# Layer 1's FFN down projection as seven products of halves in three groups, in a two-layer decoder kernel

## The chip, the cores and the metric

The kernel runs on one core of a Trainium2 chip. The metric is device time in microseconds of one execution, the median of several runs. All numbers of the trace come from one execution of the kernel, taken by the hardware profiler.

## The reference

Two decoder layers on 512 tokens of width 1024, float32. Each layer has a mixer (four parallel branches, lifted, gated and summed, then an output projection with a residual) and a feed-forward network (FFN). The change concerns the FFN of the second layer (layer 1), above all its last product:

```python
hf = rmsnorm(x, norm_ffn)
gate, up = jnp.split(hf @ ffn_w_up, 2, axis=-1)      # 1024 -> 2 x 2816
return x + (jax.nn.silu(gate) * up) @ ffn_w_down     # 2816 -> 1024
```

## The kernel before

**Precision.** Every large product is made of three matmuls: each operand is split into a high part (`_hi`, a rounded copy made by ScalarE, ACT) and a low part (`_lo`, the difference, made by VectorE, DVE), and `mm3` (L271, matmuls on L274 to L276) adds hi x hi, hi x lo and lo x hi into one PSUM bank. Weights come from DRAM by the queue of SyncE (SP) into two raw tiles of 128 x 2048 (`w_raw`). `Chunk` (L212) issues the load and splits it into parts of 128 x 1024; `w_hi` and `w_lo` have three buffers each, so that the splits run at most three parts ahead of TensorE (PE). PSUM's eight banks are three `mm`, three `tr` and two `at`.

**The FFN** (`ffn`, L1058) works in two parts: hidden columns 0 to 1535 (six chunks of 256) and 1536 to 2815 (five chunks). For each chunk, `features` computes gate and up with the weights as the stationary operand and the 512 tokens streaming; DVE scales the banks by the norm `r_b`, ACT applies Silu, DVE multiplies, and the result is split into `a_hi`, `a_lo` (L1087, L1088): twelve or ten k-tiles of 128 hidden columns. Then the part's down projection follows, so the stages of an FFN are up 0, down 0, up 1, down 1.

**Down projections.** In layer 0, and in part 0 of layer 1, `residual` (L1020) computes two output blocks of 128 columns at a time, with weights stationary, and adds the banks to `xT`, the residual stream in transposed form, which stays in SBUF from the mixer's output projection on. In part 0 of layer 1 the finished `xT` is also transposed by PE into `x_tok` (`transposed`, L1064). In part 1 of layer 1, `final` (L1043) has tokens as the output's partitions: `a` is stationary, 512 weight columns stream, four banks hold four tiles of 128 tokens, and the banks are added to `x_tok` and written out, the last 512 columns in halves on the SP and ACT queues.

**Order.** Each engine works through its own queue in order. The order in each queue was fixed when the program was built: instructions are placed as their inputs become ready by the builder's plan, those under `tc.high_priority` first (the splits of weights have `AHEAD`), and dependencies added by hand (`add_manual_dep`) are kept. The pool of `w_raw` has two buffers, so a load waits until both parts of the load two before it are split.

Of the kernel before, what the change touches and what calls it, by code (L numbers as in the profile page):

```python
# [12 lines left out]
F32 = mybir.dt.float32  # L13
# [8 lines left out]
P = 128  # L22
# [47 lines left out]
def hybrid_trunk(ctx: ExitStack, tc: tile.TileContext, x, mem, positions, norm_mix, w_in, conv_w,  # L70
# [43 lines left out]

    ident = consts.tile([P, P], F32, name="ident")
# [11 lines left out]
    neg = consts.tile([P, P], F32, name="neg")  # L127
# [143 lines left out]
    def mm3(ps, a, b, first, last):  # L271
        ah, al = a
        bh, bl = b
        pe.matmul(ps, ah, bh, start=first, stop=False)  # L274
        pe.matmul(ps, ah, bl, start=False, stop=False)  # L275
        pe.matmul(ps, al, bh, start=False, stop=last)  # L276
# [26 lines left out]
    def column_means(ps, ones, sq, hi, lo):  # L303
        A(hi, sq, AF.Copy)
        dve.tensor_sub(lo, sq, f(hi))
        pe.matmul(ps, ones, hi, start=True, stop=False)
        pe.matmul(ps, ones, lo, start=False, stop=True)

    def norm_feature(ssq):
        ps = tr_ps()  # L310
        column_means(ps, ones_dr, ssq, *(scratch512(S).bitcast(F32R) for _ in range(2)))
        r = state.tile([P, S], F32, name="rstd", bufs=1)
        rstd(r, ps, scratch512(S), scratch512(S))
        return r
# [170 lines left out]
    ones_dr = consts.tile([P, P], F32R, name="ones_dr")  # L485
    dve.tensor_copy(ones_dr, ones_d)
# [8 lines left out]
    mx, e0, e1, sm, z0 = (small(H4, name=f"lb{i}", bufs=1) for i in range(5))  # L495
# [20 lines left out]
    def mixer(l, h, norms, cm, cf):  # L516
# [176 lines left out]
        with pool_("dsa") as dp:  # L693
# [46 lines left out]
            with pool_("idx") as ip:  # L740
# [83 lines left out]
                def select(t):  # L824
# [12 lines left out]
                    dve.copy_predicated(score[:, t * P:], future, neg)  # L837
# [23 lines left out]
                mgp = cf.enter_context(pool_("mgp", "left"))  # L861
# [142 lines left out]
        res = cf.enter_context(tc.tile_pool(name="res", bufs=1))  # L1004
# [13 lines left out]
        return h2, ssq2, xT  # L1018

    def residual(xT, w2d, a, kt, cols, h2, ssq2, gain, spill=False, done=None):  # L1020
        for m0 in range(0, KD, cols // P):
            ws = []
            k0 = 0
            per = 2048 // cols
            while k0 < kt:
                n = min(per, kt - k0)
                ws.append((k0, n, wchunk(w2d[k0 * P:(k0 + n) * P, m0 * P:m0 * P + cols], n, cols)))
                k0 += n
            pss = [mm_ps() for _ in range(cols // P)]
            for js in ([range(cols // P)] if m0 + cols // P < KD else [[j] for j in range(cols // P)]):  # L1030
                for k0, n, w in ws:
                    features(w, a, js, k0, kt, [pss[j] for j in js])
            for j in range(cols // P):
                m = m0 + j
                dve.tensor_add(xT[:, m, :], xT[:, m, :], pss[j])
                if h2 is not None:
                    h_chunk(h2, ssq2, m, gain(m), xT[:, m, :])
                if spill:
                    nc.scalar.dma_start(x_dram[:, m, :], xT[:, m, :])
                if done is not None:  # L1040
                    done(m)

    def final(x_tok, w2d, a, kt):  # L1043
        for m0 in range(0, D, 512):
            cols = slice(m0, m0 + 512)
            ws = [wchunk(w2d[k0 * P:min(k0 + 4, kt) * P, cols], min(4, kt - k0), 512) for k0 in range(0, kt, 4)]
            pss = [mm_ps() for _ in range(MM_BUFS)] + [at_ps()]
            tokens_wide(ws, a, kt, pss)
            for t, ps in enumerate(pss):
                for c in ([cols] if m0 == 0 else [slice(m0 + e, m0 + e + 256) for e in (0, 256)]):  # L1050
                    dve.tensor_add(x_tok[:, t, c], x_tok[:, t, c], ps[:, c.start - m0:c.stop - m0])
                    if m0:
                        q = nc.sync if c.start == m0 else nc.scalar
                        q.dma_start(out[0][t * P:(t + 1) * P, c], x_tok[:, t, c])
            if m0 == 0:
                nc.sync.dma_start(out[0][:, cols].rearrange("(t p) c -> p t c", p=P), x_tok[:, :, cols])

    def ffn(l, h, ssq, xT):  # L1058
# [5 lines left out]
        def transposed(m):  # L1064
            ps = tr_ps()
            for t in range(NT):
                pe.transpose(ps[:, t * P:(t + 1) * P], xT[:, m, t * P:(t + 1) * P], ident)
            A(x_tok[:, :, m * P:(m + 1) * P], ps.rearrange("p (a b) -> p a b", b=P), AF.Copy)

        with tc.tile_pool(name="ffn", bufs=1) as fp:  # L1070
            for f0, f1 in parts:
                kt = 2 * (f1 - f0)
                a = (fp.tile([P, 12, S], F32R, name="a_hi")[:, :kt], fp.tile([P, 12, S], F32R, name="a_lo")[:, :kt])
                for fc in range(f0, f1):
                    wg = wchunk(ffn_w_up[l][:, fc * 256:(fc + 1) * 256], KD, 256)
                    wu = wchunk(ffn_w_up[l][:, FF + fc * 256:FF + (fc + 1) * 256], KD, 256)
                    gs = [fp.tile([P, S], F32, name="fg", bufs=2) for _ in range(2)]
                    us = [fp.tile([P, S], F32, name="fu", bufs=2) for _ in range(2)]
                    for w, dsts in ((wg, gs), (wu, us)):
                        for dst, ps in zip(dsts, features(w, h, (0, 1))):  # L1080
                            dve.tensor_mul(dst, ps, r_b)  # L1081
                    for j in range(2):
                        i = 2 * (fc - f0) + j
                        g, u = gs[j], us[j]
                        A(g, g, AF.Silu)
                        dve.tensor_mul(g, g, u)  # L1086
                        A(a[0][:, i, :], g, AF.Copy)  # L1087
                        dve.tensor_sub(a[1][:, i, :], g, f(a[0][:, i, :]))  # L1088
                wd = ffn_w_down[l][f0 * 256:f1 * 256, :]
                h2 = ssq2 = None  # L1090
                if last and f1 == n_f:
                    final(x_tok, wd, a, kt)
                    continue
                if f1 == n_f:
                    h2, ssq2 = new_h(), new_ssq()
                if last:
                    x_tok = fp.tile([P, NT, D], F32, name="x_tok")
                residual(xT, wd, a, kt, 256, h2, ssq2, lambda c: g_mix(l + 1, c), spill=h2 is not None,
                         done=transposed if last else None)
        return h2, ssq2  # L1100

    for l in range(DEPTH):
        with ExitStack() as ctx_ffn:
            with ExitStack() as ctx_mix:
                h, ssq, xT = mixer(l, h, (lambda: (norm_token(ssq), norm_feature(ssq))) if l else (lambda: norms),
                                   ctx_mix, ctx_ffn)
            h, ssq = ffn(l, h, ssq, xT)
# [29 lines left out]
```

## Time and profile before

| | us |
|---|---|
| median of three runs | 2047.89 (2046.0 to 2048.18) |
| the profiled execution's own time | 2047.71 |
| its span, first to last instruction | 2045.6 |
| PE busy | 2031.7 (99%) |
| DVE busy | 1277.0 (62%) |
| ACT busy | 1019.9 (50%) |
| GpSimd (POOL) busy | 9.8 (0%) |
| mean granted clock of PE | 0.997 |

Rows of a view name the line of the kernel, the engine, the operation, output <- inputs by the program's names, sizes and counts. PE is matmuls, PEld the loading of their stationary operands. A matmul's length in a row is pipelined, so the spacing of starts, not the length, is its price.

### The profile page before, as it was taken

To read this page: it belongs to the slowest core of one execution; us is meant where nothing else is said; L and a number is where in the kernel's file an instruction comes from. 1 tells how busy PE (TensorE), PEld (TensorE's weight loads), DVE (VectorE), ACT (ScalarE), POOL (GpSimd) and SP (SyncE) were. 2 spreads that over 40 slices of the span, in tenths; PEclk is the share of its full clock that TensorE was granted. 3 is DMA by queue.
4 is the path that set the end of the run, shared out by engine and by line. 5 is a ranking of instruction groups with operands and counts; after the bars stand their busy time and mean duration, and the time that the engine had idled before them with its cause. 6 is when DMAs were issued, how large, how long until landed. Compare 5 with 4: busy or idle time off the path is not lost.

```text
span 2045.6 us, 26194 instructions
## 1 busy us (share of the span) xinstructions
PE 2031.7 (99%) x10156; PEld 1705.9 (83%) x10156; DVE 1277.0 (62%) x2519; ACT 1019.9 (50%) x1836; POOL 9.8 (0%) x33
## 2 busy tenths in 40 slices
PE   8999999999999999999999999999999999999999
PEld 8998987778888888888889898877888788888887
DVE  6779997657686544344457889864777654533442
ACT  7653655866665433223355456486766633322231
POOL 0000000000000000000000000000000000000000
PEclk9999999999999999999999999999999999999999
DMA  7623232212243232233243213222222422323222
GB/s 251 221 85 97 68 103 83 81 54 93 68 128 113 83 103 93 93 104 102 88 155 94 88 57 108 88 62 83 83 83 83 145 87 98 103 73 113 92 83 93
DMA packets 185660, 203.77 MB, mean 100 GB/s; under 512 B 4271, under 2 KB 172289, under 8 KB 185409
## 3 DMA queue, kind: packets, MB, share of 16 engines
q1 hardware_dynamic: 181248, 193.04, 29.7%
q10 hardware_dynamic: 4128, 8.93, 1.2%
q8 instruction: 80, 1.31, 0.3%
q14 instruction: 44, 0.35, 0.1%
q0 software_dynamic: 160, 0.13, 0.0%
HBM read 191.60 MB, written 10.49 MB: 99 GB/s over the span
## 4 chain that ended last, share of the span: by engine, by line
PE 97%; DMA 1%; DVE 1%; ACT 1%; issue 0%; SPq 0%; DVEq 0%
PE mm L274 29%; PE mm L275 29%; PE mm L276 29%; PE tr L732 1%; PE tr L726 1%; PE at L702 1%; PE at L703 1%; PE at L276 1%; PE at L274 1%; PE at L275 1%; DMA w_raw<-in_mem_w_kv_dram 1%; PE at L954 0%; PE at L980 0%; PE tr L668 0%; PE tr L771 0%
## 5 line engine op out<-in xcount | busy, mean ns | idle before, releaser
L229 DVE TENSOR_TENSOR w_lo<-w_raw,w_hi 128x1024 fp32r<-128x1024 f32 (+1 forms) x346 | 419.5, 1213 | 383.2 <-ACT w_hi L97 383.0
L274 PE MATMUL mm<-h_hi,w_hi 128*128 128x512 f32 x1664 | 651.9, 393 | 0.7 <-DVE fg L1081 0.4
L275 PE MATMUL mm<-h_lo,w_hi 128*128 128x512 f32 x1664 | 651.6, 392 | 0.0
L276 PE MATMUL mm<-h_hi,w_lo 128*128 128x512 f32 x1664 | 649.8, 392 | 0.0
L97 ACT ACTIVATE w_hi<-w_raw 128x1024 fp32r<-128x1024 f32 (+1 forms) x346 | 363.2, 1051 | 463.2 <-PE mm L275 397.5
L274 PEld LDWEIGHTS mm<-h_hi,w_hi 128*128 128x128 f32 x1664 | 313.2, 188 | 65.0 <-DVE fg L1081 1.2
L276 PEld LDWEIGHTS mm<-h_hi,w_lo 128*128 128x128 f32 x1664 | 312.9, 188 | 64.6 <-issue 0.6
L275 PEld LDWEIGHTS mm<-h_lo,w_hi 128*128 128x128 f32 x1664 | 313.1, 188 | 63.3 <-issue 1.0
L276 PE MATMUL mm<-w_hi,h_lo 128*128 128x256 f32 (+2 forms) x368 | 109.5, 298 | 0.0
L275 PE MATMUL mm<-w_lo,h_hi 128*128 128x256 f32 (+2 forms) x368 | 109.1, 297 | 0.0
L274 PE MATMUL mm<-w_hi,h_hi 128*128 128x256 f32 (+2 forms) x368 | 108.3, 298 | 0.0
L275 PE MATMUL mm<-a_lo,w_hi 128*128 128x512 f32 x272 | 106.1, 390 | 0.0
L274 PE MATMUL mm<-a_hi,w_hi 128*128 128x512 f32 x272 | 105.9, 389 | 0.0
L276 PE MATMUL mm<-a_hi,w_lo 128*128 128x512 f32 x272 | 105.6, 390 | 0.0
L274 PE MATMUL mm<-y_hi,w_hi 128*128 128x512 f32 x256 | 100.4, 393 | 1.2 <-ACT y_hi L97 1.2
L275 PE MATMUL mm<-y_lo,w_hi 128*128 128x512 f32 x256 | 100.7, 393 | 0.0
L276 PE MATMUL mm<-y_hi,w_lo 128*128 128x512 f32 x256 | 100.3, 392 | 0.0
L97 ACT ACTIVATE a_hi<-fg 128x512 fp32r<-128x512 f32 x44 | 27.8, 633 | 106.9 <-DVE fg L1086 106.9
L97 ACT ACTIVATE prob<-prob,small 128x256 f32<-128x256 f32 (+3 forms) x128 | 69.0, 554 | 14.7 <-DVE small L715 8.6
L275 PEld LDWEIGHTS mm<-w_lo,h_hi 128*128 128x128 f32 x368 | 70.2, 191 | 2.2
L276 PEld LDWEIGHTS mm<-w_hi,h_lo 128*128 128x128 f32 x368 | 70.2, 191 | 1.9
L274 PEld LDWEIGHTS mm<-w_hi,h_hi 128*128 128x128 f32 x368 | 69.9, 191 | 1.9
(377 smaller groups left out, 2982.9 us busy)
## 6 DMA issues: line engine op xcount, KB each, us to landing
w_raw<-in_w_in_dram SPq DMA_DIRECT2D x72, 1024.0 KB, 5.2
w_raw<-in_ffn_w_up_dram SPq DMA_DIRECT2D x44, 1024.0 KB, 5.1
w_raw<-in_w_lift_dram SPq DMA_DIRECT2D x32, 512.0 KB, 3.5
w_raw<-in_ffn_w_down_dram SPq DMA_DIRECT2D x16, 1024.0 KB, 5.3
w_raw<-in_mem_w_kv_dram SPq DMA_DIRECT2D x8, 1024.0 KB, 5.4
w_raw<-in_w_out_dram SPq DMA_DIRECT2D x8, 1024.0 KB, 5.4
w_raw<-in_ffn_w_down_dram SPq DMA_DIRECT2D x10, 512.0 KB, 3.4
kv<-kv ACTq DMA_DIRECT2D x8, 512.0 KB, 3.2
```

Of the source, the lines that this page charges most:

```text
L97: i = act.activation(dst, src, func, **kw)
L229: dve.tensor_sub(lo, raw[:, k:e], f(hi))
L274: pe.matmul(ps, ah, bh, start=first, stop=False)
L275: pe.matmul(ps, ah, bl, start=False, stop=False)
L276: pe.matmul(ps, al, bh, start=False, stop=last)
L702: pe.matmul(ps, q[:, hh, s], k[0][:, :n], start=True, stop=False)
L703: pe.matmul(ps, q[:, hh, s], k[1][:, :n], start=False, stop=True)
L726: pe.transpose(pp[:, (2 * e + i) * P:(2 * e + i + 1) * P], probs[2 * i + e][:, b * P:(b + 1) * P], ident)
L732: pe.matmul(pv[e * HD:(e + 1) * HD, :], vt[:, b, :], pt[:, b, e * 2 * P:(e + 1) * 2 * P], start=b == 0, stop=b == t)
```

## The change

In layer 1's FFN both parts of the down projection are computed by a seven-product scheme for 2 x 2 blocks. The blocks of the activations are two halves of the tokens (256 each) by the two k-tiles of a pair; the blocks of the weights are the same two k-tiles by two halves of the output columns (`C1`, `C2`, 512 each). Part 0 has six pairs of k-tiles, part 1 five.

- `operands` takes the place of the plain split of a chunk: it stores hi and lo of seven blocks of 256 tokens, A11, A12, A22 and the sums S1 to S4.
- `down` runs three groups over all pairs. The first takes the weight blocks as they are, the second three sums of blocks, the third one sum and one plain block; each group loads its weights again. Per pair and product two tiles of 128 tokens are multiplied by 512 columns: 12, 18 and 12 matmuls of 512 columns a pair. The results collect in six banks (`ba`, `bb`, `bc`), which between the groups are added to `acc` (the token-major residual) and go on accumulating or start anew.
- Of the three sums of weights in a pair of the second group, two are on GpSimd (`pool.tensor_sub`) and one on DVE, in place in the raw tile; the third group's sum is on GpSimd. A third raw tile, `w_raw7`, joins the two.
- `follow` orders the additions of banks ahead of later splits on DVE.
- `x_in` loads the residual from DRAM on GpSimd's queue and transposes it into `acc` during the up stage of part 0.
- `xT` no longer stays in SBUF during the FFN: the mixer's `residual` writes it to DRAM, and layer 0's FFN (`add_down`) loads chunks `x_c` on GpSimd's queue, adds and writes back.
- Smaller constants (`neg`, one matrix of ones less, small tiles shared), a spacer of 128 bytes at the front of SBUF, and waits for reused memory by tile instead of by pool in the FFN.

The matmuls of `down` pass `skip_group_check` through `mm3`. The core of the diff follows, of the FFN the lines that stand after the change (what they replace is in the listing above):

```diff
+    consts.tile([P, 128], U8, name="spacer")
...
-    neg = consts.tile([P, P], F32, name="neg")
+    neg = consts.tile([P, 1], F32, name="neg")
...
-    def column_means(ps, ones, sq, hi, lo):
-        A(hi, sq, AF.Copy)
-        dve.tensor_sub(lo, sq, f(hi))
+    def column_means(ps, ones, sq, hi, lo, scale=1.0):
+        A(hi, sq, AF.Copy, scale=scale)
+        dve.scalar_tensor_tensor(lo, sq, scale, f(hi), op0=OP.mult, op1=OP.subtract)
...
-        res = cf.enter_context(tc.tile_pool(name="res", bufs=1))
+        res = cm.enter_context(pool_("res", "left"))
...
+    def add_down(x_chunk, w2d, a, kt, h2, ssq2, gain):
+        for m0 in range(0, KD, 2):
+            ws = [(k0, wchunk(w2d[k0 * P:min(k0 + 8, kt) * P, m0 * P:(m0 + 2) * P], min(8, kt - k0), 256))
+                  for k0 in range(0, kt, 8)]
+            xs = [x_chunk(m0 + j) for j in range(2)]
+            pss = [mm_ps() for _ in range(2)]
+            for js in ([range(2)] if m0 + 2 < KD else [[0], [1]]):
+                for k0, w in ws:
+                    features(w, a, js, k0, kt, [pss[j] for j in js])
+            for j, xc in enumerate(xs):
+                m = m0 + j
+                dve.tensor_add(xc, xc, pss[j])
+                    h_chunk(h2, ssq2, m, gain(m), xc)
+                nc.scalar.dma_start(x_dram[:, m, :], xc)
+
+    HALF = S // 2
+    A11, A12, A22, S2, S1, S4, S3 = range(7)
+    C1, C2 = slice(512, 1024), slice(0, 512)
+
+    def raw_tile(fp, turn=[0]):
+        turn[0] += 1
+        if turn[0] % 3 == 0:
+            return fp.tile([P, 2048], F32, name="w_raw7")
+        return wpool.tile([P, 2048], F32, name="w_raw", bufs=RAW_BUFS)
+
+    def follow(i, earlier):
+        for e in earlier:
+            tc.add_manual_dep(i.ins, e.ins.name, order, reason="additions first")
+
+    def split(src, earlier=()):
+
+        n = src.shape[1]
+        hi, lo = (wpool.tile([P, 1024], F32R, name=nm, bufs=W_BUFS)[:, :n * 512].rearrange("p (k n) -> p k n", n=512)
+                  for nm in ("w_hi", "w_lo"))
+        with tc.high_priority(offset=AHEAD):
+            A(hi, src, AF.Copy)
+            follow(dve.tensor_sub(lo, src, f(hi)), earlier)
+        return [(hi[:, k, :], lo[:, k, :]) for k in range(n)]
+
+    def operands(fp, g0, g1):
+
+        hi, lo = (fp.tile([P, 7, HALF], F32R, name=nm, bufs=6) for nm in ("a_hi", "a_lo"))
+
+        def put(o, n, src):
+            h_, l_ = (x[:, o:o + n, :].rearrange("p a b -> p (a b)") for x in (hi, lo))
+            A(h_, src, AF.Copy)
+            dve.tensor_sub(l_, src, f(h_))
+
+        put(A11, 1, g0[:, :HALF])
+        put(A12, 2, g1)
+        dve.tensor_add(g0[:, HALF:], g0[:, HALF:], g1[:, HALF:])
+        dve.tensor_sub(g0[:, :HALF], g0[:, HALF:], g0[:, :HALF])
+        both = g1.rearrange("p (a b) -> p a b", b=HALF)
+        dve.tensor_sub(both, both, g0[:, None, :HALF].to_broadcast([P, 2, HALF]))
+        put(S2, 2, g0)
+        put(S4, 2, g1)
+        return hi, lo
+
+    def down(fp, w2d, ops, evict):
+
+        n = len(ops)
+        b0 = mm_ps()
+        ba, bb, bc = [mm_ps(), mm_ps()], [b0, tr_ps()], [at_ps(), at_ps()]
+
+        def prod(bank, i, o, b, start, stop, more=False):
+            hi, lo = ops[i]
+            for t, ps in enumerate(bank):
+                s = slice(t * P, (t + 1) * P)
+                mm3(ps, (hi[:, o, s], lo[:, o, s]), b, start, stop, more)
+
+        for i0 in range(0, n, 2):
+            m = min(2, n - i0)
+            raw = raw_tile(fp)[:, :m * 1024].rearrange("p (k n) -> p k n", n=512)
+            nc.sync.dma_start(raw, w2d[2 * i0 * P:2 * (i0 + m) * P, C1].rearrange("(k p) n -> p k n", p=P))
+            for i in range(m):
+                p1, p2 = split(raw[:, 2 * i:2 * i + 2, :])
+                prod(ba, i0 + i, A11, p1, i0 + i == 0, i0 + i == n - 1)
+                prod(bb, i0 + i, A12, p2, i0 + i == 0, i0 + i == n - 1)
+        added = evict(ba, 0, C1) + evict(bb, 0, C1, True)
+        for i in range(n):
+            raw = raw_tile(fp)
+            nc.sync.dma_start(raw.rearrange("p (e n) -> p e n", e=2),
+                              w2d[2 * i * P:2 * (i + 1) * P, :].rearrange("(e p) n -> p e n", p=P))
+            earlier = added if i else ()
+            with tc.high_priority(offset=AHEAD):
+                pool.tensor_sub(raw[:, 512:1024], raw[:, :512], raw[:, 512:1024])
+                follow(dve.tensor_sub(raw[:, 1024:1536], raw[:, 1024:1536], raw[:, 512:1024]), earlier[:2])
+                pool.tensor_sub(raw[:, 1536:], raw[:, 1536:], raw[:, 1024:1536])
+            p5, p6 = split(raw[:, 512:1536].rearrange("p (k n) -> p k n", n=512), earlier)
+            p4, = split(raw[:, 1536:].rearrange("p (k n) -> p k n", n=512), earlier)
+            todo = [(bc, S1, p5, i == 0, False), (ba, S2, p6, False, True), (bb, A22, p4, i == 0, False)]
+            for bank, o, p, first, more in ([todo[1], todo[0], todo[2]] if i == n - 1 else todo):
+                prod(bank, i, o, p, first, i == n - 1, more)
+        added = evict(ba, 0, C2) + evict(bc, 2, C2)
+        later = added + evict(bb, 2, C1)
+        late = []
+        for i0 in range(0, n, 2):
+            m = min(2, n - i0)
+            raw = raw_tile(fp)[:, :m * 1024].rearrange("p (k n) -> p k n", n=512)
+            nc.sync.dma_start(raw, w2d[2 * i0 * P:2 * (i0 + m) * P, C2].rearrange("(k p) n -> p k n", p=P))
+            with tc.high_priority(offset=AHEAD):
+                pool.tensor_sub(raw[:, 0::2, :], raw[:, 1::2, :], raw[:, 0::2, :])
+            for i in range(m):
+                k = i0 + i
+                p7, p3 = split(raw[:, 2 * i:2 * i + 2, :], added if k == 1 else later if k else ())
+                prod(ba, k, S3, p7, False, k == n - 1, True)
+                late.append((bc, k, S4, p3, False, k == n - 1, True))
+                if k != n - 2:
+                    for q in late:
+                        prod(*q)
+                    late = []
+        evict(ba, 2, C2, True)
+        evict(ba, 2, C1, True)
+        evict(bc, 0, C2, True, True)
+
...
+        with tc.tile_pool(name="ffn", bufs=1, reuse_waits="tile") as fp:
+            def x_chunk(m):
+                xc = fp.tile([P, S], F32, name="x_c", bufs=4)
+                nc.gpsimd.dma_start(xc, x_dram[:, m, :])
+                return xc
+
+            def x_in(m0):
+                xs = fp.tile([P, 2048], F32, name="w_raw7")
+                nc.gpsimd.dma_start(xs.rearrange("p (m t) -> p m t", t=S), x_dram[:, m0:m0 + 4, :])
+                for m in range(4):
+                    ps = tr_ps()
+                    for t in range(NT):
+                        pe.transpose(ps[:, t * P:(t + 1) * P], xs[:, m * S + t * P:m * S + (t + 1) * P], ident)
+                    A(acc[:, :, (m0 + m) * P:(m0 + m + 1) * P], ps.rearrange("p (a b) -> p a b", b=P), AF.Copy)
+
+            h2 = ssq2 = None
+            for part, (f0, f1) in enumerate(parts):
+                ops = []
+                if not last:
+                    kt = 2 * (f1 - f0)
+                    a = (fp.tile([P, 12, S], F32R, name="a_hi")[:, :kt], fp.tile([P, 12, S], F32R, name="a_lo")[:, :kt])
                 for fc in range(f0, f1):
                     wg = wchunk(ffn_w_up[l][:, fc * 256:(fc + 1) * 256], KD, 256)
                     wu = wchunk(ffn_w_up[l][:, FF + fc * 256:FF + (fc + 1) * 256], KD, 256)
+                    gs = [fp.tile([P, S], F32, name="fg", bufs=3) for _ in range(2)]
                     us = [fp.tile([P, S], F32, name="fu", bufs=2) for _ in range(2)]
                     for w, dsts in ((wg, gs), (wu, us)):
                         for dst, ps in zip(dsts, features(w, h, (0, 1))):
                             dve.tensor_mul(dst, ps, r_b)
+                    for g, u in zip(gs, us):
                         A(g, g, AF.Silu)
                         dve.tensor_mul(g, g, u)
+                    if not last:
+                        for j, g in enumerate(gs):
+                            i = 2 * (fc - f0) + j
+                            A(a[0][:, i, :], g, AF.Copy)
+                            dve.tensor_sub(a[1][:, i, :], g, f(a[0][:, i, :]))
+                        continue
+                    ops.append(operands(fp, *gs))
+                    if fc == 0:
+                        acc = fp.tile([P, NT, D], F32, name="acc")
+                    if fc in (1, 3):
+                        x_in(2 * fc - 2)
+                final = part == len(parts) - 1
                 wd = ffn_w_down[l][f0 * 256:f1 * 256, :]
+                if not last:
+                    if final:
+                        h2, ssq2 = new_h(), new_ssq()
+                    add_down(x_chunk, wd, a, kt, h2, ssq2, lambda c: g_mix(l + 1, c))
                     continue
+
+                def evict(bank, t0, cols, done=False, tail=False):
+                    tail = final and tail
+                    adds = []
+                    with tc.high_priority(offset=2 * AHEAD):
+                        for t, ps in enumerate(bank):
+                            for w in (slice(0, 256), slice(256, 512)) if tail else (slice(0, 512),):
+                                c = slice(cols.start + w.start, cols.start + w.stop)
+                                d = acc[:, t0 + t, c]
+                                adds.append(dve.tensor_add(d, d, ps[:, w]))
+                                if final and done:
+                                    q = nc.scalar if tail and w.start else nc.sync
+                                    q.dma_start(out[0][(t0 + t) * P:(t0 + t + 1) * P, c], d)
+                    return adds
+
+                down(fp, wd, ops, evict)
```

90 lines of the change are left out of this document (19 added, 71 removed).

## The prediction

> **What bounds the kernel now.** I read the page's head, busy table and chain first.
>
> ```profile
> span 2045.6 us, 26194 instructions
> PE 2031.7 (99%) x10156; PEld 1705.9 (83%) x10156; DVE 1277.0 (62%) x2519; ACT 1019.9 (50%) x1836; POOL 9.8 (0%) x33
> PE 97%; DMA 1%; DVE 1%; ACT 1%; issue 0%; SPq 0%; DVEq 0%
> ```
>
> TensorE is both the busiest engine and 97% of the chain. A busy PE needn't be at its peak, so I asked by stage (columns: stretch, its length, busy us and instructions of PE, PEld, DVE, ACT, POOL, then granted clock, DMA share, GB/s). The last five are layer 1's FFN: up 0, down 0, up 1, down 1, tail.
>
> ```profile
> 40.00:400.00 360.00, 358.72 (x2073) 311.68 (x2072) 285.63 (x788) 214.59 (x486) 1.39 (x6) 1.00 0.34 108
> 1030.00:1340.00 310.00, 308.83 (x1717) 268.25 (x1716) 247.10 (x642) 167.87 (x373) 1.38 (x6) 1.00 0.31 97
> 1340.00:1600.00 260.00, 258.83 (x1286) 210.06 (x1285) 170.86 (x296) 180.32 (x318) 1.49 (x4) 1.00 0.25 78
> 1687.00:1820.00 133.00, 132.80 (x586) 109.64 (x585) 62.65 (x74) 43.54 (x52) 0.00 (x0) 1.00 0.29 95
> 1820.00:1886.00 66.00, 66.00 (x309) 54.61 (x308) 20.20 (x20) 17.29 (x20) 0.00 (x0) 1.00 0.29 96
> 1886.00:1990.00 104.00, 104.00 (x460) 86.14 (x459) 49.35 (x59) 31.87 (x38) 0.00 (x0) 1.00 0.30 96
> 1990.00:2030.00 40.00, 40.00 (x178) 33.11 (x177) 11.86 (x13) 8.06 (x8) 0.00 (x0) 1.00 0.27 93
> 2030.00:2046.00 16.00, 11.64 (x52) 9.30 (x50) 3.01 (x8) 0.00 (x0) 0.00 (x0) 1.00 0.19 66
> ```
>
> Both down stages run PE without a hole, at full clock, with DVE about 30% busy. A product left out there is time won, as long as the other engines keep up. Its price is the spacing of matmuls in the last stage (columns: start, length, what):
>
> ```profile
> 2028.78 0.39 PE L275 MATMUL mm<-w_lo,a_hi 128*128 128x512 f32 x1
> 2041.25 0.39 PE L276 MATMUL at<-w_hi,a_lo 128*128 128x512 f32 x1
> 2041.68 0.75 DVE L1051 TENSOR_TENSOR x_tok<-x_tok,at 128x256 f32<-128x256 f32 x2 [0.61 <-PE at L276]
> ```
>
> 55 issues lie between the first two: 12.47 / 55 = 0.2267 us each (the 0.39 is a pipelined length). The 1886:1990 row agrees: 104 / 460 = 0.226.
>
> **What the change removes.** The down projection's matmuls in the groups by shape (count, busy, mean ns):
>
> ```profile
> L275 PE MATMUL mm<-a_lo,w_hi 128*128 128x512 f32 x96 | 37.7, 393 | 0.0
> L274 PE MATMUL mm<-w_hi,a_hi 128*128 128x512 f32 x60 | 23.3, 389 | 0.0
> L274 PE MATMUL at<-w_hi,a_hi 128*128 128x512 f32 x20 | 7.8, 389 | 0.0
> L1067 PE MATMUL tr<-ident,xT 128*128 128x128 f32 x32 | 4.8, 272 | 0.0
> ```
>
> Three lines each: 3 x 176 = 528. After: 42 per pair of k-tiles, 11 pairs, 462. So 66 fall away: 66 x 0.2267 = **15.0 us**. The 32 transposes stay; they move into the up stage, where the first waits for a POOL-queue load of four x chunks spilled four chunks (over 20 us of PE) before the FFN. I cost it at nothing.
>
> **What it adds, against PE's time.** Durations of the helpers:
>
> ```profile
> L229 DVE TENSOR_TENSOR w_lo<-w_raw,w_hi 128x1024 fp32r<-128x1024 f32 x62 | 76.0, 1225 | 133.3 <-ACT w_hi L97 133.3
> L97 ACT ACTIVATE w_hi<-w_raw 128x1024 fp32r<-128x1024 f32 x62 | 65.8, 1061 | 139.7 <-PE mm L275 111.4 <-PE at L276 19.8 <-PE mm L276 8.5
> L1088 DVE TENSOR_TENSOR a_lo<-fg,a_hi 128x512 fp32r<-128x512 f32 x22 | 15.2, 692 | 14.7 <-ACT a_hi L97 14.7
> L97 ACT ACTIVATE a_hi<-fg 128x512 fp32r<-128x512 f32 x22 | 13.9, 633 | 53.6 <-DVE fg L1086 53.6
> L1035 DVE TENSOR_TENSOR xT<-xT,mm 128x512 f32<-128x512 f32 x8 | 5.5, 688 | 15.6 <-PE mm L276 15.6
> L1051 DVE TENSOR_TENSOR x_tok<-x_tok,mm 128x256 f32<-128x256 f32 x6 | 2.3, 418 | 11.1 <-PE mm L276 11.1
> L879 POOL MEMSET a_intra<- 128x512 f32 x4 | 2.0, 524 | 0.0
> L589 POOL MEMSET gate<- 128x2 f32 x8 | 0.7, 102 | 180.2 <-DVE gate L602 180.1
> L132 POOL TENSOR_SCALAR_AFFINE_SELECT causal_bias<-causal_bias 128x128 f32<-128x128 f32 x1 | 0.3, 307 | 0.0
> ```
>
> *A subtraction on GpSimd (p).* No row shows one. MEMSET writes at (524 - 102) / 510 = 0.83 ns an element; the select, which also reads, takes (307 - 102) / 128 = 1.6. If the second operand's read hides, 512 elements take 0.10 + 512 x 1.6 ns = 0.92 us; if reads add up (0.77 each), 0.10 + 512 x 2.37 ns = 1.32. Far end 1.8 (twice the select's rate). I take 1.32, since adding up is what the two rows do. [...]
>
> *Operands.* Per up chunk DVE has a_lo 4 instead of 2 and three sums: 0.42 + 3 x 0.69 + 2 x 0.42 + 0.69 = 4.0 us instead of 1.4; ACT 2.3 instead of 1.3. Of a chunk's 96 x 0.2267 = 21.8 us that takes DVE from 47% to 60%: nothing on the path.
>
> *First group,* 12 matmuls a pair, 2.72 us: ACT 1.06, DVE 1.23. Covered.
>
> *Second group,* 18 matmuls, 4.08 us: ACT 1.06 + 0.63; DVE 1.23 + 0.69 (splits) + 0.69 (sum) = 2.61; POOL 2p = 2.64. Each alone fits. The hand-over: the additions of four banks stand ahead of the next pair's split on DVE: 3 x 0.69 for two banks and one sum, 2 x 0.69, 0.69, 1.23 = 5.4 us from the moment the first bank is done, 1.4 us before the group ends, so ready 4.0 us into it. PE asks for that split 24 matmuls in, at 5.4 us. Covered by 1.4 us; the banks themselves are asked for later than they are emptied.
>
> *Third group,* 12 matmuls, 2.72 us: DVE 1.23, POOL p = 1.32. In DVE's order the first split of this group stands ahead of the additions; its buffer comes free 18 matmuls (4.1 us) before the second group ends, so it is ready 4.1 - 1.06 - 1.23 = 1.8 us before. Five additions then end 1.65 us into the group and the next split at 2.9; PE asks for it after 18 matmuls, at 4.1. Covered by 1.2 us.
>
> *Weights come twice* (23 MB instead of 11.5).
>
> ```profile
> q1 hardware_dynamic: 181248, 193.04, 29.7%
> w_raw<-in_ffn_w_down_dram SPq DMA_DIRECT2D x16, 1024.0 KB, 5.3
> xin<-in_x_dram SPq DMA_DIRECT2D x2, 1024.0 KB, 9.8
> ```
>
> The queue moves 193.04 MB in 29.7% of 2045.6 us: 318 GB/s when busy. The second group asks for 1.05 MB per 4.08 us, 257 GB/s. One raw tile's round: landing 5.3, sums p + 0.69 + p, split 0.63 + 0.69, together 10.0 us; three tiles give 3.3 us a pair, under 4.08. It is the tightest cover: when it tears, every pair waits.
>
> For these covers of 1 to 2 us I allow waits of **2.5 us** in both parts (0 to 5: up to 0.45 in each of 11 pairs).
>
> *Tail.* The order built has the last pair's matmuls interleaved over four banks, so two banks end 6 and 4 matmuls before the end and DVE then has four additions of 0.69 and four of 0.38 (0.75 a pair): from 1.36 us before the last matmul, 4.3 us, ending 2.9 us after it. Now the last two, 0.75 us, start as it ends: **+2.2 us**, up to 3.2 if the 1.6 MB written behind it (4.9 us at 318 GB/s) land last; much less is excluded, since one engine does all eight.
>
> *Elsewhere* layer 0's FFN reads x chunks by the POOL queue and spills on ACT's; at most two transfers of 256 KB per 30 matmuls (6.8 us), beside a DMA share of 0.29: nothing. The x loads stand ahead of the first sum on POOL's queue and are over long before it. The smaller constants, the broadcast `neg` and the scale in `column_means` leave their instructions' shapes as they were: nothing. The instruction order in the mixers shifts; their holes (1.28 + 1.17 + 1.17 us in the rows above) bound that: 0, within 2 either way.
>
> **Sum.** The profiled execution took 2047.7 us (span 2045.6 and 2.1 around it; median of the runs 2047.9). 2047.7 - 15.0 + 2.5 + 2.2 = 2037.4, put on the median **2037.6 us**. Its own range is 2033 (no waits, mixers 2 better) to 2043 (all upper ends).
>
> **Rivals.** *Shared reading (33%).* DVE's subtractions with both inputs in SBUF and GpSimd's sums do not run beside each other. For it: nothing in the trace has the two engines on such work together (POOL 9.8 us in all), so it is untested; against it: nothing either, so one chance in three. [...] Price: a pair of the second group then needs 2.61 + 2p = 5.25 us of one resource, not 4.08. Per part: n x 5.25, four additions 2.76, split and sum ahead of the third group 1.23 + 2.64, less what was done before (one pair's work and a sum, 6.6), against 4.08 n: 7.0 us late for n = 6, 5.9 for n = 5; two additions that stand behind (1.4) and one sum in the first hand-over (1.3) per part make 18 us. 2047.7 - 15.0 + 18 + 2.2 = **2053**: slower. Each 0.1 us of p moves it by 2: at 0.92 it gives 2045, at 1.8 2062. It turns slower from p = 1.07.
>
> *The transfers bind (8%).* Landing is 9.8 us where two megabytes come at once (xin row). Round 14.5 us, 4.83 a pair, 0.75 x 11 = 8.3 instead of 2.5: 2043. For: 257 of 318 GB/s; against: 5.3 us landing in the median.
>
> *It gives back elsewhere (4%).* Mixer holes double, 3.6 us: 2041; with more, no change. That the matmuls do not fall away is excluded: the order built has 462.
>
> **Numbers.** Forecast 55%. About 0.2% (4 us) is what a measurement can tell from no change: faster is under 2043.8, slower over 2052. Faster: 52 of the forecast's 55, 5 of the transfers, 2 of elsewhere, 3 of shared reading (small p): 62%. Same: 3, 3, 2 and 7: 15%. Slower: 23%, shared reading at p over 1.27. Range 2034 to 2054: it takes in the rivals up to p = 1.37 and leaves out some 15%, most of it above.
>
> **What would show it.** Right: 462 down matmuls at 0.227 us; PE over 95% busy in both down stages, now 252 and 210 matmuls, 57.1 and 47.6 us, plus waits; w_lo still near 1225 ns where POOL is busy; POOL sums spaced under 1.4 us. Shared reading: w_lo or the sums stretched (a mean over 1.5 us) in the second group, PE waiting there for w_lo and at the third group's start for DVE. Transfers: the sums waiting for w_raw's DMA. Wrong altogether: holes outside layer 1's FFN.

## The result, and the profile after

The changed kernel took 2056.5 us (median of 5 runs, 2053.9 to 2058.1) against 2047.9 (2046.0 to 2048.2): a ratio of 1.0042 [1.0028, 1.0057], slower where a gain of 10 us was forecast. The profiled execution took 2056.78 us, of which its span is 2055.1, 9.5 us longer than before's.

The page's head and chain, then the same stretches as before (the last row is longer, since the span is):

```profile
span 2055.1 us, 26424 instructions
PE 2027.8 (99%) x10090; PEld 1698.9 (83%) x10090; DVE 1359.8 (66%) x2620; ACT 1048.5 (51%) x1880; POOL 70.9 (3%) x79
PE 92%; DVE 3%; DMA 2%; POOL 1%; ACT 1%; issue 1%; SPq 0%; DVEq 0%; POOLq 0%; ACTq 0%
```

```profile
40.00:400.00 360.00, 355.73 (x2044) 309.69 (x2043) 283.44 (x795) 209.32 (x476) 1.38 (x6) 0.99 0.33 107
1340.00:1600.00 260.00, 260.00 (x1295) 211.49 (x1295) 172.51 (x301) 182.24 (x325) 1.49 (x4) 1.00 0.26 82
1820.00:1886.00 66.00, 61.16 (x257) 48.50 (x256) 52.14 (x52) 24.36 (x27) 27.78 (x15) 0.97 0.50 172
1886.00:1990.00 104.00, 104.00 (x461) 86.11 (x460) 58.26 (x77) 35.27 (x45) 0.00 (x0) 1.00 0.31 99
1990.00:2030.00 40.00, 37.66 (x163) 29.90 (x161) 33.99 (x34) 15.67 (x19) 21.82 (x12) 1.00 0.58 204
2030.00:2056.00 26.00, 16.41 (x60) 13.04 (x60) 13.73 (x19) 3.18 (x3) 1.90 (x2) 0.78 0.19 71
```

66 matmuls are gone (10156 to 10090). But PE now has holes in both down stages, DVE is at 79% and 85% there (52.14 / 66, 33.99 / 40) where it was at 30%. The granted clock is 0.97 in the row of down 0 and 0.78 in the last row, which holds the end of down 1; before, it was 1.00 in both. The two down parts cut exactly, from the first matmul to the end of the last:

```profile
1818.48:1883.83 65.35, 60.52 (x253) 47.97 (x252) 51.25 (x49) 24.36 (x27) 27.78 (x15) 0.97 0.51 176
1992.63:2048.61 55.98, 51.28 (x211) 40.77 (x209) 43.27 (x43) 18.43 (x21) 23.72 (x13) 0.94 0.39 140
```

462 matmuls at 0.2267 us need 104.7 us; the parts took 121.3. **16.6 us are lost there.** The groups by shape say what became slow:

```profile
L230 DVE TENSOR_TENSOR w_lo<-w_raw,w_hi 128x1024 fp32r<-128x1024 f32 x316 | 385.8, 1223 | 293.4 <-ACT w_hi L97 292.8
L1068 DVE TENSOR_TENSOR w_lo<-w_raw,w_hi 128x1024 fp32r<-128x1024 f32 x33 | 46.4, 1407 | 17.8 <-ACT w_hi L97 17.7
L1068 DVE TENSOR_TENSOR w_lo<-w_raw,w_hi 128x512 fp32r<-128x512 f32 x11 | 16.7, 1519 | 1.1 <-ACT w_hi L97 1.1
L1117 POOL TENSOR_TENSOR w_raw<-w_raw 128x512 f32<-128x512 f32 x11 | 18.0, 1639 | 236.4 <-DMA w_raw<-in_ffn_w_down_dram 236.4
L1119 POOL TENSOR_TENSOR w_raw<-w_raw 128x512 f32<-128x512 f32 x11 | 18.8, 1707 | 8.4 <-DVE w_raw L1118 8.4
```

One sum with no subtraction beside it on DVE (timeline: start, length, what):

```profile
2006.38 1.29 POOL L1117 TENSOR_TENSOR w_raw<-w_raw 128x512 f32<-128x512 f32 x1 [6.88 <-DMA w_raw<-in_ffn_w_down_dram]
```

The split of 128x512, 0.69 us when alone (e1 and e2 below), takes 1.52 in the second group; the sums, 1.29 alone, average 1.64 and 1.71. How they lengthen each other is seen at the third group's start:

```profile
1861.59 2.37 POOL L1133 TENSOR_TENSOR w_raw<-w_raw 128x1024 f32<-128x1024 f32 x1 [0.75 <-DMA w_raw<-in_ffn_w_down_dram]
1861.96 3.08 DVE L1068 TENSOR_TENSOR w_lo<-w_raw,w_hi 128x1024 fp32r<-128x1024 f32 x1 [0.58 <-ACT w_hi L97]
1864.97 1.27 DVE L1212 TENSOR_TENSOR acc<-acc,mm 128x512 f32<-128x512 f32 x2
1865.79 0.47 PE L275 MATMUL mm<-w_hi,a_hi 128*128 128x512 f32 x1 [3.15 <-DVE acc L1212]
1866.81 2.38 POOL L1133 TENSOR_TENSOR w_raw<-w_raw 128x1024 f32<-128x1024 f32 x1 [2.85 <-DMA w_raw<-in_ffn_w_down_dram]
1867.36 0.67 DVE L1212 TENSOR_TENSOR acc<-acc,mm 128x512 f32<-128x512 f32 x1
1867.96 2.31 DVE L1068 TENSOR_TENSOR w_lo<-w_raw,w_hi 128x1024 fp32r<-128x1024 f32 x1
```

Both splits end 1.08 us after the sum beside them (1863.96 to 1865.04, 1869.19 to 1870.27): they stand while the sum runs and do their work behind it (1.22 us in L230's group above). The addition of a PSUM bank in between, with one input in SBUF, takes its usual 0.67 beside the same sum (20 of them average 0.68). And while the split stands, the additions behind it on DVE stand too, and PE waits 3.15 us for them.

These two holes cost more than themselves. The hole and the stretch after it, in part 0 and in part 1:

```profile
1862.20:1865.80 3.60, 0.45 (x3) 0.05 (x2) 3.60 (x3) 1.74 (x2) 1.76 (x1) 1.00 0.77 279
1867.10:1870.50 3.40, 3.40 (x10) 2.63 (x9) 3.40 (x4) 0.00 (x0) 2.09 (x1) 0.51 0.00 0
2028.60:2032.40 3.80, 0.43 (x3) 0.07 (x1) 3.80 (x3) 1.60 (x2) 2.95 (x2) 0.81 0.43 138
2032.40:2037.80 5.40, 5.40 (x13) 4.23 (x14) 5.07 (x7) 0.00 (x0) 0.35 (x1) 0.50 0.00 0
```

After each of the two PE works at half its clock, its matmuls 0.43 us apart instead of 0.2267: 3.4 us long in part 0 and 5.4 in part 1 (there it begins in the hole, at 2031.0, and is 6.8 long in all): (3.4 + 5.4) / 2 = 4.4 of the 16.6 us. What PE waited for, from the list for the whole run (us in total, times, longest):

```profile
PE mm L275 <- DVE acc L1212: 6.5, 2, 3.4
PE at L701 <- DVE small L714: 5.1, 6, 3.1
PE at L276 <- DVE w_lo L1068: 1.8, 3, 0.8
PE mm L276 <- DVE w_lo L1068: 0.8, 2, 0.6
```

The second line lies in layer 0's mixer, far from the products. Before, it was:

```profile
PE at L702 <- DVE small L715: 2.4, 6, 0.4
```

Last, the end:

```profile
2048.38 0.39 PE L277 MATMUL at<-w_hi,a_lo 128*128 128x512 f32 x1
2049.84 1.41 DVE L1212 TENSOR_TENSOR acc<-acc,at 128x256 f32<-128x256 f32 x4
```

DVE is done 2.9 us after the last matmul's start and the span ends 6.7 after it, against 4.35 before: +2.4. The ledger of the profiled executions: -15.0 + 16.6 + 2.4 leaves 9.5 - 4.0 = **5.5 us that are lost outside layer 1's down parts.** Two places stand out in the trace:

```profile
338.00:344.80 6.80, 6.61 (x19) 5.50 (x20) 4.45 (x14) 2.98 (x11) 0.00 (x0) 0.50 0.25 76
1324.40:1327.80 3.40, 3.40 (x10) 2.63 (x10) 3.40 (x6) 2.73 (x10) 0.00 (x0) 0.50 0.02 4
```

The wait at L701 is 2.7 us longer than before, and the half clock behind it lasts 6.8 us instead of 3.4 (336.0 to 339.4 before). A stretch of 3.4 us in layer 1's mixer is new. That is 2.7 + 1.7 + 1.7 = 6.1 us, about the 5.5.

### The profile page after: what moved, and what is told of

It is laid out like the page before. It is cut to its first block, busy times and chain, and to the rows that moved or that the text cites. A ratio compares the mean times of both kernels' runs of the same rounds, so it can differ in the third digit from the quotient of the medians.

```text
span 2055.1 us, 26424 instructions
## 1 busy us (share of the span) xinstructions
PE 2027.8 (99%) x10090; PEld 1698.9 (83%) x10090; DVE 1359.8 (66%) x2620; ACT 1048.5 (51%) x1880; POOL 70.9 (3%) x79
## 3 DMA queue, kind: packets, MB, share of 16 engines
q8 instruction: 79, 1.29, 0.3%
## 4 chain that ended last, share of the span: by engine, by line
PE 92%; DVE 3%; DMA 2%; POOL 1%; ACT 1%; issue 1%; SPq 0%; DVEq 0%; POOLq 0%; ACTq 0%
PE mm L275 28%; PE mm L276 28%; PE mm L277 28%; DMA w_raw<-in_ffn_w_down_dram 1%; PE tr L731 1%; PE at L701 1%; PE at L702 1%; PE tr L725 1%; PE at L275 1%; DVE w_lo L1068 1%; PE at L277 1%; PE at L276 1%; DMA w_raw<-in_mem_w_kv_dram 1%; ACT w_hi L97 0%; POOL w_raw L1117 0%
## 5 line engine op out<-in xcount | busy, mean ns | idle before, releaser
L97 ACT ACTIVATE w_hi<-w_raw 128x1024 fp32r<-128x1024 f32 (+2 forms) x368 | 381.5, 1039 | 446.2 <-PE mm L276 336.1
L230 DVE TENSOR_TENSOR w_lo<-w_raw,w_hi 128x1024 fp32r<-128x1024 f32 (+1 forms) x324 | 392.5, 1213 | 298.3 <-ACT w_hi L97 297.6
L97 ACT ACTIVATE a_hi<-fg 128x512 fp32r<-128x512 f32 (+1 forms) x66 | 39.4, 597 | 107.4 <-DVE fg L1184 91.2
L1068 DVE TENSOR_TENSOR w_lo<-w_raw,w_hi 128x1024 fp32r<-128x1024 f32 (+1 forms) x44 | 62.5, 1435 | 18.8 <-ACT w_hi L97 18.8
L275 PE MATMUL mm<-a_hi,w_hi 128*128 128x512 f32 x176 | 68.5, 389 | 0.0
L276 PE MATMUL mm<-a_lo,w_hi 128*128 128x512 f32 x176 | 68.5, 389 | 0.0
```

What stands on the lines that cost most here:

```text
L97: i = act.activation(dst, src, func, **kw)
L230: dve.tensor_sub(lo, raw[:, k:e], f(hi))
L275: pe.matmul(ps, ah, bh, start=first, stop=False, skip_group_check=more)
L276: pe.matmul(ps, ah, bl, start=False, stop=False, skip_group_check=more)
L1068: follow(dve.tensor_sub(lo, src, f(hi)), earlier)
```

## The experiments

*Loss* is the length of both down parts less the spacing of their matmuls, from each run's profile. The kernel before ran beside each set of runs (medians 2046.6 to 2047.9).

| | median us | ratio to before | loss us |
|---|---|---|---|
| changed kernel | 2056.5 | 1.0042 [1.0028, 1.0057] | 16.6 |
| e1 sums on DVE | 2044.0 | 0.9986 [0.9976, 0.9996] | 3.8 |
| e2 writes only | 2040.3 | 0.9964 [0.9951, 0.9977] | 0.6 |
| e3 own small tiles | 2052.9 | 1.0027 [1.0018, 1.0037] | 14.2 |
| e4 = e1 + e3 | 2045.2 | 0.9989 [0.9979, 0.9998] | 5.7 |
| e5 plain product | 2051.0 | 1.0021 [1.0011, 1.0031] | 0.0 |
| e6 third's sums on DVE | 2049.3 | 1.0011 [1.0002, 1.0021] | 10.0 |
| e7 second's sums on DVE | 2044.3 | 0.9985 [0.9975, 0.9995] | 4.5 |
| e8 = e1, additions first | 2043.9 | 0.9987 [0.9977, 0.9996] | 2.9 |
| e9 hole filled | 2053.7 | 1.0031 [1.0020, 1.0043] | 5.5 |
| e10 = e1, tail's order | 2043.8 | 0.9985 [0.9976, 0.9994] | 5.3 |
| e11 = e1, all orders | 2040.1 | 0.9964 [0.9950, 0.9978] | 0.6 |
| e12 = e11 on GpSimd | 2051.4 | 1.0019 [1.0010, 1.0028] | 14.4 |

(In e9 the loss leaves out the 6.8 us of its added matmuls.)

**Is it the reading?** e1:

```diff
-  pool.tensor_sub(raw[:, 512:1024], ...)        # and L1119, L1133
+  dve.tensor_sub(raw[:, 512:1024], ...)
```

> Edit: the three kinds of weight sums (L1117, L1119, L1133) are done by VectorE instead of GpSimd; nothing else. Theory A (VectorE's two-input subtractions and GpSimd's sums hold each other up; in the changed kernel w_lo then takes a mean of 1435 ns with single ones of 3.4 us, and PE waits 16.6 us in the two down parts, the slowed clock behind two of these holes included): with no GpSimd work left w_lo is back at 1.22 to 1.23 us, a sum costs VectorE 0.69 us, a pair of the second group 3.99 us of VectorE against 4.08 us of PE, so waits of 3 to 8 us stay in both parts and the time is 2044 to 2049. Theory B (the down weights' transfers, landing late, hold the parts up): the sums start when their data has landed as before, time 2055 to 2059. Theory C (VectorE is full: 3.99 of 4.08 us with the accumulators' additions on top): waits as long as now, 2055 to 2062, with PE waiting for w_lo at its normal length.

e2:

```diff
-  pool.tensor_sub(raw[:, 512:1024], raw[:, :512], raw[:, 512:1024])
+  pool.memset(raw[:, 512:1024], 0.01)
+  pool.memset(raw[:, 512:1024], 0.01)
+  pool.memset(raw[:, 512:640], 0.01)            # the other sums alike
```

> Edit: each GpSimd sum is replaced by writes of a constant over the same destination, 2.25 times its length, so that GpSimd is busy about as long at the same place (estimate from the write's rate of 0.83 ns an element: 1.15 us for a sum of 512, which takes 1.29 us alone) and everyone waits for it as before, but it reads nothing. The sums' values are lost. Theory A (reads on both sides exclude each other): w_lo back at 1.23 us, the GpSimd writes unstretched, waits in the down parts fall from 16.6 us to 0 to 5, time 2040 to 2046. Theory D (GpSimd's place in the chain, its length and the hand-overs to and from it, cost the time, whatever it does): within 3 us of 2056.5.

e1 gave 2044.0, A's lower end; B and C, 2055 and more, fall. The groups of e1 and then of e2:

```profile
L1068 DVE TENSOR_TENSOR w_lo<-w_raw,w_hi 128x1024 fp32r<-128x1024 f32 x33 | 39.9, 1219 | 13.8 <-ACT w_hi L97 13.8
L1068 DVE TENSOR_TENSOR w_lo<-w_raw,w_hi 128x512 fp32r<-128x512 f32 x11 | 7.5, 686 | 1.2 <-ACT w_hi L97 1.2
L1117 DVE TENSOR_TENSOR w_raw<-w_raw 128x512 f32<-128x512 f32 x11 | 7.6, 687 | 1.5 <-DMA w_raw<-in_ffn_w_down_dram 1.5
```

```profile
L1068 DVE TENSOR_TENSOR w_lo<-w_raw,w_hi 128x512 fp32r<-128x512 f32 x11 | 7.6, 689 | 4.7 <-ACT w_hi L97 4.6
L1117 POOL MEMSET w_raw<- 128x512 f32 x11 | 5.8, 531 | 244.0 <-DMA w_raw<-in_ffn_w_down_dram 230.2 <-issue 8.3 <-DVE w_lo L1068 4.4
1816.81:1873.93 57.12, 57.12 (x253) 47.30 (x252) 40.05 (x49) 24.58 (x27) 19.98 (x45) 1.00 0.60 202
1982.73:2030.99 48.26, 48.10 (x211) 39.07 (x209) 33.49 (x43) 18.53 (x21) 16.75 (x39) 1.00 0.46 163
```

In e2 GpSimd is nearly as busy at the same places (three writes of 0.53, 0.52 and 0.20 us for a sum of 1.29) and everyone still waits for it, but it reads nothing: the split is back at 0.69 and the parts run without a hole. So neither GpSimd's own length nor its place in the chain costs the time (D falls), nor the transfers, which move the same bytes, but its reading beside DVE's two-input subtractions. (e2 takes away the arithmetic together with the reading. That the reading matters fits the rows above, where an addition with one input in SBUF ran beside such a sum at its usual 0.67 us.) e1 costs less than the sums on GpSimd although DVE has more to do.

**Where is the lateness made?** e6 moves only L1133 to DVE, e7 only L1117 and L1119 (edits as in e1).

> Edit: only the third group's sums (L1133) are on VectorE; the second group's two stay on GpSimd. Theory A2 (the two holes of over 3 us at the third group's start come from the long sum L1133, 2.4 to 3.4 us, beside the split that stands ahead of the additions on VectorE): these holes shrink to under 1.5 us and no slow clock follows them; the smaller waits in the second group (about 2 us in each part) stay: 2056.5 less 8 to 11 = 2045.5 to 2048.5. Rival H (the lateness is built up in the second group and only shows at the third's start): the holes stay over 2.5 us and the time is 2053 to 2057.

> Edit: only the second group's sums (L1117, L1119) are on VectorE; the third group's (L1133) stay on GpSimd. Theory A2: the second group's waits go or stay small, the holes at the third group's start stay over 2 us with slow clock behind: 2049 to 2054. Rival H: the holes go, 2044 to 2047.

The waits of PE in the down parts, e6 and then e7:

```profile
PE mm L275 <- DVE acc L1212: 2.9, 2, 1.5
PE mm L276 <- DVE w_lo L1068: 2.3, 4, 0.9
PE at L276 <- DVE w_lo L1068: 1.8, 3, 0.7
```

```profile
PE mm L276 <- DVE w_lo L1068: 1.8, 3, 0.9
PE mm L275 <- ACT w_hi L97: 0.5, 1, 0.5
PE mm L275 <- DVE acc L1212: 0.2, 1, 0.2
```

e7 (2044.3) is H's case: with the second group's sums off GpSimd the holes go, though the third group's still collide, here with GpSimd as the one that stands (3.34 us where it took 2.37 above):

```profile
1853.99 1.23 DVE L1068 TENSOR_TENSOR w_lo<-w_raw,w_hi 128x1024 fp32r<-128x1024 f32 x1
1854.13 3.34 POOL L1133 TENSOR_TENSOR w_raw<-w_raw 128x1024 f32<-128x1024 f32 x1 [122.65 <-DVE w_raw L1119]
```

e6 is nearer to A2's case: the holes at the third group's start shrink to 1.5 us, no slow clock shows behind them (in part 0 the next matmuls start 0.23 us apart, and the profile's mean granted clock is 0.996, the changed kernel's 0.992), and H's 2053 is not reached. But its 2049.3 lies just above A2's range, and a loss of 10.0 stays. So the long sum L1133 makes the holes as long as they are, and the second group makes the lateness without which they don't appear. The third group has room to take turns in (1.23 + 1.3 of 2.72 us a pair), the second has not (2.61 + 2.6 of 4.08). That lateness shows where the order on DVE puts the additions behind a split.

**Was it the order?** e8 orders the third group's later sums behind the additions:

```diff
-  dve.tensor_sub(raw[:, 0::2, :], ...)
+  follow(dve.tensor_sub(raw[:, 0::2, :], ...), added if i0 else ())
```

> Edit: all sums on VectorE, as in the run before, and the third group's later sums are ordered behind the additions of ba and bc (in that run such a sum, waiting 0.7 us for its data and taking 1.2, stood ahead of the additions, and PE waited 1.3 us for them). If that order is the cause: the wait of 1.3 us goes, time 2041.5 to 2043.5. If the split that follows only becomes late instead: 2043.5 to 2045.

2043.9: the wait for the additions went (1.3 to 0), the waits for splits grew (0.7 to 2.1 in all), the second of the two outcomes. e10 orders the tail:

```diff
-  prod(*q)
+  prod(*q, earlier=[e] if k == n - 1 else ())   # e: ba's last matmul
```

> Edit: on top of all sums on VectorE (2044.0), the last two pairs' products into bc are ordered behind the last one into ba in each part, so that ba's four additions run beside bc's last 12 matmuls (2.7 us) instead of standing behind the last matmul; matmuls and additions stay as many. Theory K (the end is set by VectorE's additions behind the last matmul, ba's four of 0.6 to 0.68 and bc's four of 0.41): the time from the last matmul to the end falls from 6.7 us by 1 to 1.5: 2042.5 to 2043. Rival L (the writes of the output set the end): no change, 2043.5 to 2044.5.

The last matmul now is 5.8 us from the end instead of 6.7 (2036.76 to 2042.5), a little less than K expected. The median, 2043.8, is the one that L expected, but not for L's reason: a wait for a split in the third group grew from 0.7 to 2.2 us and took the gain back. The two orders have to be mended together, e11 (on top of e10):

```diff
+  follow(<sum L1133>, added if i0 == 2 else los[1:2])     # los: the group's splits
-  later = added + evict(bb, 2, C1)
-  p7, p3 = split(..., added if k == 1 else later if k else ())
+  p7, p3 = split(..., added if k else ())
+  if k == 2: for i in evict(bb, 2, C1): follow(i, los)
```

> Edit: all sums on VectorE, the tail's order as in the run before it, and at the third group's start VectorE does the additions of ba and bc first, then a sum and a split in turn; bb's two additions, which nobody waits for, stand behind the third split. If VectorE's order at that start was what was left of the waits (1.3 + 0.7 us, or 2.1 with the additions alone moved): 2040 to 2042. If it only moves them: 2042.5 to 2044.

```profile
1819.87:1876.99 57.12, 57.12 (x254) 47.31 (x252) 50.68 (x66) 24.35 (x27) 0.00 (x0) 1.00 0.60 201
1985.79:2034.00 48.21, 48.03 (x211) 38.92 (x209) 42.64 (x58) 18.54 (x21) 0.00 (x0) 1.00 0.46 167
```

2040.1, 0.36% under before: with DVE 89% busy in these rows, PE waits 0.2 us in both parts together. Of the versions that compute the result it is the fastest. e12 is e11 with the sums back on GpSimd.

> Edit: the version of e11 (VectorE's order at the third group's start, bb's additions late, the tail's order) with all three kinds of sums back on GpSimd: against the changed kernel only the orders differ, against e11 only the engine of the sums. Theory A (VectorE's two-input subtractions and GpSimd's sums take turns, so a pair of the second group needs about 2.6 + 2.6 us of one resource against 4.08 us of PE): w_lo and the sums are stretched as in the changed kernel, the waits in the second group and at the third's start stay, 2049 to 2056. Rival M (the orders were the fault, not the engine): 2040 to 2044.

2051.4, in A's range: the orders alone are worth 5 us, the engine of the sums 11. M, which expected 2044 at most, falls.

**What the slow clock costs.** e9, in the changed kernel:

```diff
+  fill = tr_ps()
+  fills = [pe.matmul(fill, <128x128>, <128x512>, start=True, stop=True) for _ in range(15)]
+  # ordered behind the second group's last products and ahead of the third's first
```

> Edit: the changed kernel with 15 matmuls of 128x512 that nobody reads (15 x 0.2267 = 3.4 us of PE, into a free bank, operands that are long there) between the second and the third group of both parts, where PE stands still for 3.1 and 3.4 us. VectorE's and ScalarE's orders are unchanged. Theory I (the granted clock falls to half, in pieces of 3.4 us, after PE has stood still in such a hole, and each such piece costs 1.7 us): the hole is filled at little cost, the pieces at 1867 (one) and 2031 (two) vanish, and the kernel with more matmuls is faster: 2056.5 less 2 to 5 = 2051.5 to 2054.5. Rival J (the slow clock follows the stretch on the other engines or the third group itself, not the standstill): slow pieces stay, time 2056 to 2060.

```profile
1862.00:1872.00 10.00, 9.55 (x42) 7.38 (x41) 9.52 (x11) 3.14 (x3) 2.41 (x1) 1.00 0.46 158
2024.00:2036.00 12.00, 12.00 (x54) 9.92 (x53) 9.69 (x11) 4.96 (x5) 4.95 (x3) 1.00 0.16 55
```

With 30 matmuls more, the clock is 1.00 in both stretches, and the two parts take 117.0 us instead of 121.3, nearly the 4.4 of the sum above: in this execution I holds. The median fell by 2.8, into I's range, but the intervals of the two ratios overlap, and the profiled execution (2051.4) is the shortest of six; the others had a mean granted clock of 0.993 to 0.996 against its 0.996, and where they were slow isn't recorded.

**The loss outside.** e5 undoes the products alone (layer 1's down parts, with their operands and additions, are plain again, all else as changed):

```diff
-  down(fp, wd, ops, evict)
+  classical(acc, wd, a, kt, final)      # tokens_wide into four banks, as `final` before
```

> Edit: the changed kernel with layer 1's down projection as a plain product again (528 matmuls, two column halves, four banks, the operand buffers of layer 0's FFN, additions into acc); everything else of the change stays: the setup, the shared small tiles, layer 0's rewritten FFN, x_in, the spacer. It prices what the change costs outside the products. Theory E (the other edits cost about 6 us, 4.3 of them at the hole and slow clock behind layer 0's selection and 1.6 of slow clock in layer 1's mixer, as the spacing of the matmuls shows beside the kernel before): 2047.5 + 4 to 7 = 2051.5 to 2054.5, with the hole of 3.1 us at L701 again. Rival G (outside the down parts the change costs nothing, the prediction's term): 2046 to 2049.

2051.0 against 2047.1: the rest of the change costs 3.9 us, just under E's range and above G's, with the same wait at L701 (longest 3.1). In its profile the clock is 1.00 from 1322 to 1330 us, so it lacks the slow stretch at 1324 us, which some runs have and others not. e3 undoes one line of the rest:

```diff
-  mx, e0, e1, sm, z0 = (small(H4) for _ in range(5))
+  mx, e0, e1, sm, z0 = (small(H4, name=f"lb{i}", bufs=1) for i in range(5))
```

> Edit: the five small tiles of the lower bounds (mx, e0, e1, sm, z0) get names and buffers of their own again, as before the change; all else as changed. In the order built, layer 0's first 900 VectorE instructions then stand as in the kernel before (898 of 900 in the same order, 636 with the changed kernel's). Theory E (sharing the 12 buffers of the small tiles moved VectorE's order in layer 0's mixer, so that the selection ends about 4 us later against PE: one hole of 3.1 us at L701 and slow clock of 6.8 us instead of 3.4 behind it): the hole falls to 0.4 us as before, time lower by 4 to 6: 2050.5 to 2052.5. Rival F (that hole is a matter of the single execution, or lost again later): within 2 us of 2056.5.

```profile
PE at L701 <- DVE small L714: 1.2, 3, 0.4
```

(Waits of PE in 325 to 345 us of e3; the changed kernel has 3.9, 3, 3.1 there.) The hole goes. The lower bounds' arithmetic, at 9 us of the trace before, starts at 73 us in the changed kernel, because its tiles now share a ring of buffers with others; all of DVE's order behind it shifts, and the last selection of layer 0 ends at 335.8 us, not 331.7. But the median is only 3.6 us lower, short of E's range and with overlapping intervals, and e4 shows that it does not add:

> Edit: the sums on VectorE and the five small tiles with buffers of their own, together. If both losses are separate and additive, its time is that of the changed kernel less both gains: 2038 to 2044 by theories A and E; 2050 to 2054 by E alone; 2055 to 2060 by neither.

2045.2, no better than e1. With the five tiles apart, time is lost elsewhere: a stretch of 630 to 690 us, at the end of layer 0's mixer, in the changed kernel and in e3:

```profile
630.00:690.00 60.00, 60.00 (x266) 49.71 (x265) 36.55 (x47) 31.35 (x43) 0.13 (x2) 1.00 0.39 132
630.00:690.00 60.00, 60.00 (x260) 48.45 (x260) 35.75 (x46) 28.36 (x39) 0.14 (x2) 1.00 0.40 132
```

Six matmuls fewer in 60 us of a busy PE at full clock. From 650 to 654 us, e3's matmuls that stream `y_hi`, `y_lo` or `mg_hi`, `mg_lo` (the branches' results and their sum) start 0.233 us apart, the changed kernel's 0.227; over the whole stretch e3's mean is 60 / 260 = 0.231, so not all of them stand that far apart. By the start of the same matmul in both profiles, e3 is 4.5 us ahead at 393 us, 1.5 ahead at 705, and 0.9 behind at 1730, after layer 1's mixer: what the hole gained is used up before the down parts begin.

Why these matmuls stand 3% wider apart stays open. DVE's order doesn't explain it: the kernel before, whose order e3 nearly restores, has 267 matmuls in this stretch. The five tiles also take 80 bytes a partition of their own, which can move other tiles to other addresses; that was not tested.

## Why the prediction was wrong

- *66 matmuls, 15.0 us:* right. e11's parts take 105.3 us for 462, against 104.7.
- *A subtraction on GpSimd, p = 1.32:* right, 1.29 us alone.
- *Second group, "Each alone fits":* this is the step that failed. DVE's 2.61 and GpSimd's 2.64 us a pair were laid beside each other; the rows show them holding each other up (a split of 0.69 us took 1.52, sums of 1.29 took 1.64 and 1.71). One after the other they make 5.2, against 4.08, and in part 0 the sums L1117 of the third to the sixth pair start 5.3 to 5.8 us apart. The "shared reading" rival named this mechanism, its place and its price, 18 us of waits; 16.6 were lost, 4.4 of them as slow clock, which it did not have. So 12.2 us were waits, and that the rival's 2053 came near 2056.5 is partly luck: the slow clock and the loss elsewhere more than made up for waits that were fewer than its 18. It got a third of the chance because no row of before tested it; "Each alone fits" rested on no such row either, so a third was too little.
- *Third group, first split "ready 1.8 us before":* wrong by the same step. In part 0 it ended at 1865.04, 2.8 us after the second group's last matmul started. The sum ahead of it took 3.4 us instead of 2.4 and it 3.08 instead of 1.23. "Covered by 1.2 us" turned into the largest holes, 3.1 and 3.4 us. Without the collision the covers are thin but hold: e2 loses 0.6 us where the forecast allowed 2.5.
- *The transfers bind:* ruled out by e2 and e11, whose raw tiles pass the same data.
- *Tail +2.2:* +2.4. DVE's end 2.9 us after the last matmul is as worked out; before, it was 1.2 us behind the last matmul's start and not 0.75, so 1.7 of the 2.4 are DVE's and the rest lies behind it.
- *Elsewhere "0, within 2":* wrong by size, 3.9 (e5) to 5.5 us. "The smaller constants ... nothing" looked at the shapes of instructions, not at their order: sharing five tiles of 16 bytes moved a selection of DVE and opened a hole of 3.1 us. What else makes up the 3.9 is not shown, since e3 lost the hole's gain again in other places.
- Put together from measured terms (the losses from the profiles, the last from e5's median): 2047.9 - 15.0 + 16.6 + 2.4 + 3.9 = 2055.8, against 2056.5.

## What to carry to other kernels

Before work is handed to GpSimd to relieve VectorE, count VectorE's instructions with two inputs in SBUF and GpSimd's instructions that read SBUF. In this kernel the two held each other up (a split of 0.69 us took 1.52 beside sums, a sum of 1.29 took 1.64 to 1.71 beside splits), and the same orders ran 11 us faster with all sums on VectorE, 89% busy there, than with them on GpSimd. When every cover is 1 to 2 us, write out the order on the engine that carries them, and put what PE waits for (bank additions) ahead of what it doesn't; mending one of two such orders only moved the wait. Edits that "change nothing" but buffers can still change the order that a builder chooses, so price them by a run with the main edit undone.

## What the runs showed of the hardware

In the changed kernel the slow clock came in pieces of 3.4 us (at 1867 and 1324 us, clock 0.51 and 0.50) and 6.8 us (at 338 and 2031 us, clock 0.50). Whether a hole draws one depends on more than its length: 3.1 and 3.4 us of waiting drew one and two in the changed kernel, while in e3 the same hole in part 0 (3.0 us) drew none:

```profile
1866.50:1872.00 5.50, 4.94 (x22) 3.79 (x21) 5.50 (x7) 1.06 (x1) 2.40 (x1) 1.00 0.07 8
```

What else it depends on, no run here shows. The 30 runs of the kernel before beside e5 lie at 2045.6 to 2046.5 (12), 2046.9 to 2047.7 (14) and 2049.3 to 2049.6 (4). Their middles are 1.3 and 2.1 us apart, near the 1.7 us that 3.4 us at half the clock cost. But three of the 25 beside e1 to e4 lie between the upper two groups, at 2048.15 to 2048.73, and the cause was not tested.
